# Two 32-expert layers of a transformer kernel: products in written order, weight slots by first release, 1664 expert slots instead of 1792

## The chip, the cores and the metric

One core of one Trainium2 chip runs the whole program in one launch. The metric is the device time of that launch in microseconds (us), as the median of several runs. The engines are PE (TensorE: products, with its weight loads as PEld), DVE (VectorE), ACT (ScalarE), POOL (GpSimd) and SP (SyncE, whose queue issues all weight transfers here). A megabyte (MB) is a million bytes.

## What is computed

The reference takes 512 tokens of width 1024 in float32. Block 1 ends in a layer of 16 experts. Block 2 has two depths, and each ends in a layer of 32 experts (4 groups of 8): a token's group is the largest group logit, its two experts are the two largest logits within it, and every expert applies `silu(x Wg) * (x Wu)` of width 512, then `Wd`. Cut to the part that the change touches:

```python
def _hier_moe(x, w_grp, b_grp, w_exp, b_exp, w_gate, w_up, w_down):
    ...
    g_idx = jnp.argmax(grp_logits, axis=-1)
    ...
    top_l, top_e = lax.top_k(in_grp, TOP_K_IN_GROUP)
    gate = p_grp[:, None] * jax.nn.softmax(top_l, axis=-1)
    eid = (g_idx[:, None] * EXPERTS_PER_GROUP + top_e).reshape(-1)
    ...
    def expert_block(args):
        idx, e = args
        xb = x_pad[idx]
        hdn = jax.nn.silu(xb @ w_gate[e]) * (xb @ w_up[e])
        return hdn @ w_down[e]
```

A layer so has 1024 pairs of token and expert, and the weights of its 32 experts are 32 x 3 x 512 x 1024 x 4 bytes, 201 MB.

## The kernel before, in words

`program()` runs block 1 (a mixer, a router, 16 experts), then twice a mixer, a router and a 32-expert layer. The two 32-expert layers share one function, `moe_sorted` (L491 to L626).

**Sorting and passes.** The number of pairs of an expert is known only on the chip. The router ranks the experts by it and writes the list `eids` (L1041): which expert stands at which place. The places are fixed ahead, by `_passes()` (L39 to L64). A place has one or two passes, and a pass is a number of rows (slots) that a product handles at once. Kind b, for the experts with the most pairs, has two passes of 64 and 32 rows; kind m has one of 64; kind s one of 32; kind f has one of 64 for an expert whose number is written in the program, so that its weights can be fetched before the list exists. Before there are `FIRST = 4` f, `BIG = 4` b, `MID = 12` m and 12 s: 36 passes, 1792 slots. Pairs that do not fit run in a loop behind the layer (`further`), whose count is read on the chip. Passes are collected into units of 128 slots (14 units), and units into groups of at most two units (7 groups).

**The weights.** All weights go through a ring of 12 slots of 1.049 MB each (`ring`, `slot()` L183, `load_w` L207). An expert needs six: gate 2, up 2, down 2, so the ring holds two experts. `fetch(x)` places expert x in slots 6x to 6x + 5, modulo 12, gate first; the fetch of expert x + 2 is written behind the last step of expert x. SP issues the transfers in this order, and its queue waits at each for the products that read the slot's old contents (L218 is the issue).

**A step.** For each pass (`step`): `pass_gates` (L652) sums the gate values of the unit's slots; `gate_up_64` (L664) or `gate_up_32` (L674) makes 64 products of 256 columns into a PSUM tile `pgu`; `hidden` applies silu and the gate; a share of `gather` (L274) collects the token columns of the next group into `xT`, 8 products for each of 8 blocks of 128; `hidden_T` (L344, L689) turns the hidden rows through the bank `ph`; the first pass of a unit then scatters the unit before (`scatter`, 8 tiles of two products at L392 into `psc`, each added to X by DVE at L395) and turns its one-hots into `ST`; `down` (L358) or `down_32` (L699) writes `py`, from where ACT and DVE copy it into a high part `Yh` (L372) and a low part `Yl` (L373).

**What sets the order.** The text order decides for SP, and within what the tile framework may move for the rest: PE's order in this function is chosen by a scheduler, which may let one step's products pass another's. `in_order()` is a context in which PE keeps the order written. The router's end, `router2`, writes `eids`, brings positions and gates into the order of passes (`by_pass`, L1062 and L1066) and works out the loop's count, all ahead of the first expert. `residual2` (L957, L958) scales X and adds a row, two DVE instructions for each of 4 token tiles; it is called from steps 0 and 1 and must precede the first scatter. `tokens2` gathers the first group's tokens ahead of the layer (L889 products, 256 columns each for four f experts; L282 and L284 modulate them into `xT`).

```python
        for x, mine in enumerate(EXPERTS):
            W = Ws[x % depth]
            ...
            for q in mine:
                step(q, W)
            fetch(x + depth)
```

Of the kernel before, what the change touches and what calls it, by code (L numbers as in the profile page):

```python
# [28 lines left out]
FIRST = 4  # L29
BIG, MID = 4, 12  # L30
# [8 lines left out]
def _passes():  # L39
# [5 lines left out]
    for g, units in enumerate((("ff", "ff"), ("bs", "mss"), ("mm", "mm"), ("bs", "mss"), ("bs", "mss"), ("mm", "mm"), ("bs", "mss"))):  # L45
        col = 0
        for u in units:
            for k in u:
                rank, low = next(kinds[k][0]), 0
                mine = []  # L50
                for size in kinds[k][1]:
                    mine.append(Pass(rank, size, low, g, unit, col))
                    col += size
                    low += size
                experts.append(mine)
                out += mine
            unit += 1
# [72 lines left out]
class Kernel:  # L130
# [57 lines left out]
    def new_ring(self):  # L188

        while self.rings:  # L190
            self.rings.pop().__exit__(None, None, None)
        for s in range(NSLOT):
            self.rings.append(self.tc.tile_pool(name=f"ring{s}", bufs=1))
            self.ring[s] = self.rings[s].__enter__()
# [12 lines left out]
    def load_w(self, src, n, inner=False):  # L207


        kt = src.shape[0] // 128  # L210
        per = SLOT // n
        out = []
        for k0 in range(0, kt, per):
            m = min(per, kt - k0)
# [46 lines left out]
    def onehot(self, g, tiles=range(NT)):  # L261

        V = self.nc.vector
        for k in tiles:
            V.tensor_tensor(self.S[g % 2][:, k].rearrange("p (e s) -> p e s", e=GRP), bc(self.c("slots"), GRP, 1),
                            bc(self.pos[:, k, g * GRP:(g + 1) * GRP], 64), OP.is_equal)
# [224 lines left out]
    def moe_sorted(self, weights, stats, finish, rows=()):  # L491
# [6 lines left out]
        depth = NSLOT // SLOTS  # L498
        last = PASSES[-1].group
        Ws = [None] * depth  # L500

        def load(e):
            W = []
            for m, w in enumerate(weights):
                w = w[e] if isinstance(e, int) else w[bass.ds(e, 1)].rearrange("o k n -> (o k) n")
                W.append(self.load_w(w, w.shape[1], m < 2))
            return W

        def fetch(x):

            if x < len(EXPERTS):
                self.wslot = SLOTS * x
# [5 lines left out]
                Ws[x % depth] = load(e)  # L518

        for x in range(depth):  # L520
            fetch(x)
        blocks = list(range(KD))

        def ahead(g, n):

            if g < last:
                for i in range(n):
                    self.gather(self.xT[(g + 1) % 2], S[(g + 1) % 2], blocks.pop(0))

        def step(q, W):  # L530
            g, i = q.group, q.i
            xq = xT[g % 2][:, :, q.col:q.col + q.size]
            if q.starts:
                blocks[:] = range(KD)
                if g < last:
                    self.onehots(g + 1)
            if q.opens and i:
                self.pass_gates(q)
            pg = self.gate_up_64(xq, W) if q.size == 64 else self.gate_up_32(xq, W)
            if i == 0:  # L540
                self.pass_gates(q)
            col = 4 * (q.unit % 2) + q.mates.index(q)
            hs = self.hidden(pg, col) if q.size == 64 else self.hidden_32(pg, col)
            n = q.size // 32 if g else (0, 2, 3, 3)[i]
            ahead(g, n // 2)
            hT = self.hidden_T(hs) if q.size == 64 else self.hidden_T_32(hs)
            if q.opens:
                if i:
                    for tt, n2 in tiles:
                        self.scatter(tt, n2, parts)  # L550
                p = self.slots_to_tokens(S[g % 2], q.col)
                nc.scalar.activation(self.ST, p, AF.Copy)
            ahead(g, n - n // 2)
            if i < 2:
                for t in (2 * i, 2 * i + 1):
                    self.residual2(t)
            r = slice(q.at, q.at + q.size)
            if q.size == 64:
                self.row = q.at // 64
                self.down(hT, W, self.Yh[r], self.Yl[r])  # L560
            else:
                self.down_32(hT, W, self.Yh[r], self.Yl[r])
# [43 lines left out]
        for x, mine in enumerate(EXPERTS):  # L606
            W = Ws[x % depth]
            if mine[0].starts and mine[0].group == last:
                self.rows = self.work[(last + 1) % 2]
                for t, r in zip(self.rows, rows):  # L610
                    self.bcast_into(t, r)
            for q in mine:
                step(q, W)
            fetch(x + depth)
        for tt, n in tiles:
            self.scatter(tt, n, parts)
# [11 lines left out]
    def onehots(self, g):  # L628

        V = self.nc.vector  # L630
        mine = [q for q in PASSES if q.group == g]
        i, n = mine[0].i, len(mine)
        for k in range(NT):
            pos = self.posp[:, k, i:i + n]
            out = self.S[g % 2][:, k]
            if n == 4:
                V.tensor_tensor(out.rearrange("p (e s) -> p e s", e=4), bc(self.c("slots"), 4, 1), bc(pos, 64), OP.is_equal)
            else:
                pos, out = pos.rearrange("p (u e) -> p u e", u=2), out.rearrange("p (u s) -> p u s", u=2)
# [2014 lines left out]
```

## Time and profile before

| | |
|---|---|
| runs | 2726.48, 2727.9, 2731.2 us; median 2727.9 |
| profiled execution | 2736.2 us; span in the trace 2734.4 us; mean granted PE clock 0.949 |
| busy PE | 2432.4 us (89%), 15602 products |
| busy PEld | 1510.4 us (55%) |
| busy DVE | 1203.9 us (44%) |
| busy ACT | 724.9 us (27%) |
| busy POOL | 284.7 us (10%) |
| transfers | 716.37 MB, mean 262 GB/s |

All positions are us from the start of the span of the one profiled execution. In the page's slices the span is cut into 40 equal parts. In a row of the trace, "64x512" is partitions x elements of the output, "x16" the number of instructions that the row collects, and what stands in brackets behind `<-` is the idle time of the engine and what ended it. "SPq" is SP's queue of transfers. A busy share is an average over stages with different limits, so a stage is read in its own window.

### The profile page before, as it was taken

To read this page: it belongs to the slowest core of one execution; us is meant where nothing else is said; L and a number is where in the kernel's file an instruction comes from. 1 tells how busy PE (TensorE), PEld (TensorE's weight loads), DVE (VectorE), ACT (ScalarE), POOL (GpSimd) and SP (SyncE) were. 2 spreads that over 40 slices of the span, in tenths; PEclk is the share of its full clock that TensorE was granted. 3 is DMA by queue.
4 is the path that set the end of the run, shared out by engine and by line. 5 is a ranking of instruction groups with operands and counts; after the bars stand their busy time and mean duration, and the time that the engine had idled before them with its cause. 6 is when DMAs were issued, how large, how long until landed. Compare 5 with 4: busy or idle time off the path is not lost. (4 is left out here: it accounts for less than half of the span.)

```text
span 2734.4 us, 39473 instructions
## 1 busy us (share of the span) xinstructions
PE 2432.4 (89%) x15602; PEld 1510.4 (55%) x15602; DVE 1203.9 (44%) x2706; ACT 724.9 (27%) x1512; POOL 284.7 (10%) x297
## 2 busy tenths in 40 slices
PE   7998996999998889998899988887978999998985
PEld 4876673443332367767666544545766755545542
DVE  4397566132221254576534333235464544333334
ACT  4452322110100043354212121114554212111111
POOL 1333231000000032110000000001440000000000
PEclk9999998999999999998899999998988999999997
DMA  7234736899999932012579999994101587989995
GB/s 264 76 112 141 252 108 239 339 409 409 409 409 409 403 120 69 24 34 95 216 310 415 397 369 392 417 366 154 46 24 35 200 332 318 417 346 407 416 367 213
DMA packets 202735, 716.37 MB, mean 262 GB/s; under 512 B 36553, under 2 KB 41577, under 8 KB 169770
## 3 DMA queue, kind: packets, MB, share of 16 engines
q1 hardware_dynamic: 202250, 713.62, 67.3%
q8 instruction: 129, 2.11, 0.3%
q14 instruction: 68, 0.56, 0.1%
q10 hardware_dynamic: 288, 0.08, 0.0%
HBM read 704.79 MB, written 8.86 MB: 261 GB/s over the span
## 5 line engine op out<-in xcount | busy, mean ns | idle before, releaser
L664 PE MATMUL pgu<-r,xT 128*64 128x256 f32 x2560 | 310.6, 390 | 0.0
L358 PE MATMUL py<-r,hT 128*64 128x512 f32 x1120 | 276.0, 619 | 15.2 <-ACT hT L346 15.1
L395 DVE TENSOR_TENSOR X<-X,psc 128x512 f32<-128x512 f32 x280 | 183.9, 685 | 204.0 <-PE psc L392 201.6
L664 PEld LDWEIGHTS pgu<-r,xT 128*64 128x64 f32 x2560 | 179.7, 139 | 107.9 <-issue 28.1
L324 PE MATMUL pgu<-r,xT 128*64 128x512 f32 x1024 | 235.2, 598 | 3.5 <-DMA r<-w_up_in 3.1
L373 DVE TENSOR_TENSOR Yl<-py,Yh 32x256 fp32r<-32x256 f32 (+1 forms) x208 | 109.1, 525 | 269.8 <-ACT Yh L372 268.6
L372 ACT ACTIVATE Yh<-py 32x256 fp32r<-32x256 f32 (+1 forms) x208 | 95.3, 458 | 306.6 <-PE py L358 151.2
L392 PE MATMUL psc<-Yh,ST 128*128 128x512 f32 x280 | 131.2, 471 | 36.6 <-ACT Yh L372 20.2
L358 PEld LDWEIGHTS py<-r,hT 128*64 128x64 f32 x1120 | 77.0, 140 | 152.0 <-issue 123.1
L1128 DVE TENSOR_TENSOR wl<-r,wh 128x512 fp32r<-128x512 f32 (+2 forms) x154 | 119.5, 790 | 91.5 <-ACT wh L1124 85.2
L1159 PE MATMUL pj<-wl,ah 128*128 128x512 f32 (+1 forms) x384 | 155.3, 405 | 2.4 <-DVE wl L1128 2.4
L1159 PE MATMUL pj<-wh,ah 128*128 128x512 f32 (+1 forms) x384 | 151.9, 415 | 5.0 <-DVE cv L1320 2.6
L1159 PE MATMUL pj<-wh,al 128*128 128x512 f32 (+1 forms) x384 | 151.0, 399 | 0.0
L324 PEld LDWEIGHTS pgu<-r,xT 128*64 128x64 f32 x1024 | 68.8, 137 | 136.8 <-issue 121.5
L1124 ACT ACTIVATE wh<-r 128x512 fp32r<-128x512 f32 (+2 forms) x168 | 97.7, 596 | 169.8 <-PE pj L1159 116.9
L274 PE MATMUL pg<-S,xh 128*128 128x256 f32 x512 | 135.6, 295 | 4.0 <-DVE xT L284 3.1
L223 POOL TENSOR_TENSOR lnmv<-lnmv,mhalf 128x1 f32<-128x1 f32 x16 | 10.4, 652 | 1235.0 <-DVE lnmv L722 1224.5
L335 ACT ACTIVATE hs<-pgu 128x256 f32<-128x256 f32 (+1 forms) x56 | 25.0, 446 | 411.4 <-PE pgu L664 274.5
L274 PE MATMUL pg<-S,xl 128*128 128x256 f32 x512 | 133.9, 292 | 0.0
L336 DVE SCALAR_TENSOR_TENSOR hs<-hs,gs,pgu 128x256 f32<-128x256 f32 (+1 forms) x56 | 31.1, 555 | 231.1 <-ACT hs L335 231.0
L674 PE MATMUL pgu<-r,xT 128*32 128x256 f32 x2048 | 126.8, 381 | 2.3 <-SPq L619 1.7
L392 PE MATMUL psc<-Yl,ST 128*128 128x512 f32 x280 | 121.6, 437 | 1.7 <-DVE Yl L373 1.3
(733 smaller groups left out, 4099.0 us busy)
## 6 DMA issues: line engine op xcount, KB each, us to landing
r<-moe_w_gate_in SPq DMA_DIRECT2D x128, 1024.0 KB
r<-moe_w_up_in SPq DMA_DIRECT2D x128, 1024.0 KB
r<-moe_w_down_in SPq DMA_DIRECT2D x128, 1024.0 KB
r<-w_down_in SPq DMA_DIRECT2D x64, 1024.0 KB
r<-w_up_in SPq DMA_DIRECT2D x64, 1024.0 KB
r<-w_gate_in SPq DMA_DIRECT2D x64, 1024.0 KB
r<-w_mod_in SPq DMA_DIRECT2D x24, 1024.0 KB
r<-ev_w_in_in SPq DMA_DIRECT2D x14, 1024.0 KB
```

Of the source, the lines that this page charges most:

```text
L274: nc.tensor.matmul(p, part[:, k, d * 128:(d + 1) * 128], S[:, k], start=(k == 0 and part is self.xh), stop=(k == NT - 1 and part is self.xl))
L324: nc.tensor.matmul(pg[64 * h:64 * h + 64, which, :], xT[:, k, j, :], w[:, h * H:(h + 1) * H], start=(k == 0 and (F == 1024 or which == 0)) ...
L358: nc.tensor.matmul(py[64 * n:64 * n + 64], hT[:, b, hf, :], w[:, n * 512:(n + 1) * 512], start=(hf == 0 and b == 0), stop=(hf == 1 and b = ...
L372: nc.scalar.activation(hi, p, AF.Copy)
L373: nc.vector.tensor_tensor(lo, p, hi.bitcast(F32), OP.subtract)
L392: nc.tensor.matmul(p, ST[:, tt * 128:(tt + 1) * 128], Y[:, n * 512:(n + 1) * 512], start=(i == 0), stop=(i == len(parts) - 1))
L395: nc.vector.tensor_tensor(a, a, p, OP.add)
L664: nc.tensor.matmul(pg[64 * h:64 * h + 64, which, :], xq[:, k], W[which][k][:, h * H:(h + 1) * H], start=(k == 0 and which == 0), stop=(k = ...
L674: nc.tensor.matmul(pg[32 * c:32 * c + 32], xq[:, k], W[1 - c // 2][k][:, c % 2 * H:(c % 2 + 1) * H], start=(k == 0), stop=(k == KD - 1), s ...
L1124: self.nc.scalar.activation(wh, w, AF.Copy)
L1128: eng.tensor_tensor(wl, w, wh.bitcast(F32), OP.subtract)
L1159: nc.tensor.matmul(banks[m], a, b, start=(k == 0 and j == 0), stop=(k == KD - 1 and j == 2))
```

## The change

The slots of a layer go from 1792 to 1664: `FIRST` 4 to 2, `BIG` 4 to 3, so there are 2 f, 3 b, 12 m and 15 s, 35 passes in 13 units. The experts from place 2 on come from the list; before, from place 4 on.

The step of a pass is split by expert into `front(x)` and `back(x)`. `front` makes gate and up of all the expert's passes side by side: the first half of the k blocks for both passes, then the second half, and it applies silu and gate. `back` turns the hidden rows, scatters the unit before with the gather blocks between its tiles (one after every two), and makes the down products. The order is front(x), back(x - 1), the fetch of down(x + 1), the fetch of gate and up of x + 2. The whole runs under `in_order()`. The gates of a unit are made behind the back that precedes it. In an expert with two passes `down_32` uses the bank `ph` in place of `py`.

The weights of gate and up are loaded as gate half 0, up half 0, gate half 1, up half 1. The slot of each load comes from a list worked out ahead (`free`): slots in the order in which the program gives them back, the four of a front behind that front, the two of a down behind its back. `new_ring(place)` lets the next mixer find its slots under this order.

In `router2` and behind it: the list is written in `numbers()`, called between the two halves of front(0); positions and gates come into pass order in `permute()`, behind front(0). The eight `residual2` instructions are called behind experts 1 and 2. The first group is gathered 128 columns wide instead of 256. The next group's one-hots are made for all four token tiles in one instruction per part.

```diff
-FIRST = 4
-BIG, MID = 4, 12
+FIRST = 2
+BIG, MID = 3, 12
...
-    for g, units in enumerate((("ff", "ff"), ("bs", "mss"), ("mm", "mm"), ("bs", "mss"), ("bs", "mss"), ("mm", "mm"), ("bs", "mss"))):
+    for g, units in enumerate((("ff",), ("mss", "mss"), ("bs", "mss"), ("mm", "mm"), ("bs", "mss"), ("mm", "mss"), ("bs", "mss"))):
...
+        def gate_up_weights(ws):
+
+            W = [[], []]
+            for k in range(0, KD, 4):
+                for m in range(2):
+                    W[m] += self.load_w(ws[m], ws[m].shape[1], True, range(k, k + 4))
+            return W
...
+        n, G = len(EXPERTS), SLOTS - SLOTS // 3
+        order = list(self.order)
+        free = list(order)
+        for x in range(n + 1):
+            free += order[SLOTS * x:SLOTS * x + G] + (order[SLOTS * x - SLOTS // 3:SLOTS * x] if x else [])
+            order += free[len(order):SLOTS * min(n, x + 3)]
+        self.freed = free[-NSLOT:]
+        self.set_order(order)
...
+        def front(x):
+
+            mine, W = EXPERTS[x], Ws[x]
+            q = mine[0]
+            if q.starts and x and q.group < last:
+                self.onehots(q.group + 1)
+            make = {64: self.gate_up_64, 32: self.gate_up_32}
+            pg = [self.mps.tile([128, 2, self.F // 2], F32, name="pgu", bufs=2) for m in mine]
+            for k in range(0, KD, 4):
+                for m, p in zip(mine, pg):
+                    make[m.size](p, xT[q.group % 2][:, :, m.col:m.col + m.size], W, range(k, k + 4))
+                if x == k == 0:
+                    self.numbers()
+            if x == 0:
+                self.permute()
+                self.onehots(1)
                 self.pass_gates(q)
...
+        def back(x, hs, blocks, g):
...
+            chores = [lambda t=t: self.scatter(*t, parts) for t in tiles] if q.opens and x else []
+            for i, d in enumerate(blocks):
+                chores.insert(3 * i + 2 if len(chores) > i else i, lambda d=d: gather(g, d))
...
+                    self.down(h, W, self.Yh[r], self.Yl[r])
+                else:
+                    self.down_32(h, W, self.Yh[r], self.Yl[r], "ph" if two else "py")
...
+        with self.in_order():
+            hs = None
+            for x, mine in enumerate(EXPERTS):
...
+                new = front(x)
+                if x:
+                    back(x - 1, hs, share.get(q.i, []), q.group + 1)
+                    fetch_down(x + 1)
+                fetch_gate_up(x + 2)
+                hs = new
+                if x in (1, 2):
+                    for t in (2 * x - 2, 2 * x - 1):
+                        self.residual2(t)
+                if x + 1 < n and EXPERTS[x + 1][0].opens:
+                    self.pass_gates(EXPERTS[x + 1][0])
+            back(n - 1, hs, [], None)
```

The order of instructions shows three places. The first is PE at the start of the first 32-expert layer. Names: `place` is the permutation, `own` belongs to the loop's count, `pos` and `gate` are the positions and gates brought into pass order, `r_` are weight slots. Before:

```order
L1040 MATMUL py<-place,C 1x36
L1062 MATMUL pg<-C,pos 32x128 x4
L1066 MATMUL pg<-place,xT_8615 128x36 x4
L1053 MATMUL py<-own,C 128x32
L1062 MATMUL pg<-C,gate 32x128 x4
L1066 MATMUL pg<-place,xT_8615 128x36 x4
L2629 UNCONDITIONAL_BRANCH
L664 MATMUL pgu<-r_8998,xT_8614 64x256 x8
L664 MATMUL pgu<-r_8999,xT_8614 64x256 x8
```

And of the change, from the last pair of the first half of expert 0 on:

```order
L722 MATMUL pgu<-r_8996,xT_8613 64x256 x2
L722 MATMUL pgu<-r_8997,xT_8613 64x256 x2
L1103 MATMUL py<-place,C 1x35
L722 MATMUL pgu<-r_8998,xT_8613 64x256 x2
L722 MATMUL pgu<-r_8999,xT_8613 64x256 x2
...
L1127 MATMUL pg<-C,pos 32x128 x4
L1131 MATMUL pg<-place,xT_8614 128x35 x4
L1127 MATMUL pg<-C,gate 32x128 x4
L1131 MATMUL pg<-place,xT_8614 128x35 x4
L1117 MATMUL py<-own,C 128x32
L711 MATMUL ph<-gate_9127,S_8615 128x4 x4
L722 MATMUL pgu<-r_9001,xT_8613 64x256 x2
```

The list's product now stands behind half of expert 0's gate and up, and the permutation behind all of it.

The second is DVE at the same place, in the change. Before, the cast into `eids` (L1041) is followed by the branch, and the residual comes within the layer:

```order
L1098 TENSOR_SCALAR own<-C,sortc 32x32
L2695 UNCONDITIONAL_BRANCH
L1043 SCALAR_TENSOR_TENSOR X<-X,resg 128x1024
L1044 SCALAR_TENSOR_TENSOR X<-resb,X 128x1024
...
L1071 MEMSET turnx 128x1
L1072 MEMSET turnx 128x1
L1104 CAST eids<-py 1x35
L1111 TENSOR_TENSOR posp<-pg,low 128x140
```

Four such pairs at L1043 and L1044 now stand ahead of the cast that SP reads its expert numbers from.

The third is PE behind an expert with 96 rows, in the change: the last scatter tile, the two downs, the turning of the one-hots (`identr`), the gates of the next unit, and the next front:

```order
L393 MATMUL psc<-Yh,ST 128x512
L393 MATMUL psc<-Yl,ST 128x512
L359 MATMUL py<-r_9001,hT 64x512 x4
L359 MATMUL py<-r_9002,hT 64x512 x4
L754 MATMUL ph<-r_9001,hT 32x256 x8
L754 MATMUL ph<-r_9002,hT 32x256 x8
L308 MATMUL psc<-identr,S_8615 128x128 x4
L711 MATMUL ph<-gate_9127,S_8615 128x6 x4
L722 MATMUL pgu<-r_8998,xT_8613 64x256 x2
```

The gates write `ph` right behind the down that wrote it, and every later product stands behind them; before, the scheduler had set 64-row gate-up products between such steps.

## Rows read from the trace of the kernel before

**Rows 1.** The page's slices of 68.4 us, the row of GB/s that the transfers moved.

```profile
GB/s 264 76 112 141 252 108 239 339 409 409 409 409 409 403 120 69 24 34 95 216 310 415 397 369 392 417 366 154 46 24 35 200 332 318 417 346 407 416 367 213
```

**Rows 2.** Windows: stretch, us, busy PE, PEld, DVE, ACT, POOL (count), PEclk, DMA, GB/s.

```profile
1349.00:1849.00 500.00, 456.50 (x3836) 259.54 (x3836) 176.71 (x396) 92.92 (x208) 0.00 (x0) 0.99 0.93 378
2194.00:2697.00 503.00, 459.48 (x3854) 260.71 (x3850) 176.49 (x397) 93.31 (x209) 0.00 (x0) 0.99 0.94 378
1440.00:1560.00 120.00, 114.88 (x892) 68.41 (x891) 43.45 (x105) 23.31 (x50) 0.00 (x0) 1.00 1.02 417
500.00:920.00 420.00, 390.71 (x1781) 149.87 (x1779) 98.25 (x174) 45.67 (x76) 0.00 (x0) 0.99 1.02 406
```

**Rows 3.** SP's longest sum of waits, 1300 to 1870 us: total us, times, longest.

```profile
SPq L218 <- PE pgu L674: 103.1, 24, 21.6
```

**Rows 4.** Timeline of SP's queue: start us, us, issues.

```profile
1347.16 2.41 SPq L218 DMA_DIRECT2D r<-moe_w_gate_in  x2
...
1407.21 2.10 SPq L218 DMA_DIRECT2D r<-moe_w_down_in  x2
1430.19 2.07 SPq L218 DMA_DIRECT2D r<-moe_w_gate_in  x2
```

**Rows 5.** Timeline of PE within the first layer: start us, us, line, operation.

```profile
1439.12 0.39 PE L274 MATMUL pg<-S,xh 128*128 128x256 f32 x1
...
1440.26 0.65 PE L664 MATMUL pgu<-r,xT 128*64 128x256 f32 x2
...
1444.08 6.69 PE L664 MATMUL pgu<-r,xT 128*64 128x256 f32 x58
...
1833.41 3.65 PE L358 MATMUL py<-r,hT 128*64 128x512 f32 x16 [0.53 <-ACT hT L346]
1836.99 3.66 PE L674 MATMUL pgu<-r,xT 128*32 128x256 f32 x64
1841.66 0.34 PE L689 MATMUL ph<-C,hs 64*128 64x64 f32 x2 [1.01 <-DVE hs L682]
1842.42 1.93 PE L699 MATMUL py<-r,hT 128*32 128x256 f32 x32 [0.43 <-ACT hT L691]
```

**Rows 6.** Timeline of PE, ACT and DVE at the start of the first layer.

```profile
1326.16 0.56 PE L889 MATMUL po<-S,xh 128*128 128x256 f32 x1
...
1331.08 0.52 PE L923 MATMUL lg<-M,onesr 128*128 128x32 f32 x4
...
1335.00 1.02 ACT L282 ACTIVATE xT<-S,pcol 128x256 f32<-128x256 f32 x2
1336.38 0.18 DVE L1041 CAST eids<-py 1x36 int32<-1x36 f32 x1 [0.37 <-PE py L1040]
1343.44 9.22 PE L664 MATMUL pgu<-r,xT 128*64 128x256 f32 x64
```

**Rows 7.** Groups by line: residual; copies of down. Busy us, mean ns, idle before.

```profile
L957 DVE SCALAR_TENSOR_TENSOR X<-X,resg 128x1024 f32<-128x1024 f32 x4 | 4.9, 1220 | 0.0
...
L373 DVE TENSOR_TENSOR Yl<-py,Yh 64x512 fp32r<-64x512 f32 x10 | 6.9, 688 | 16.1 <-ACT Yh L372 16.1
L372 ACT ACTIVATE Yh<-py 64x512 fp32r<-64x512 f32 x10 | 5.9, 592 | 19.2 <-PE py L358 15.4 <-DVE Yl L373 3.8
```

**Rows 8.** Timeline of DVE at the end of the two layers.

```profile
1864.36 1.35 DVE L395 TENSOR_TENSOR X<-X,psc 128x512 f32<-128x512 f32 x2 [0.16 <-PE psc L392]
...
2701.54 0.42 DVE L373 TENSOR_TENSOR Yl<-py,Yh 32x256 fp32r<-32x256 f32 x1 [0.44 <-ACT Yh L372]
```

**Rows 9.** Timeline of PE, the last products of the two layers.

```profile
1865.44 0.40 PE L392 MATMUL psc<-Yl,ST 128*128 128x512 f32 x1
...
2711.18 0.63 PE L392 MATMUL psc<-Yl,ST 128*128 128x512 f32 x1
```

**Rows 10.** Windows, columns as in Rows 2: the layer's start, and a stretch within it.

```profile
1320.00:1360.00 40.00, 33.01 (x188) 26.13 (x190) 25.30 (x94) 8.02 (x16) 0.00 (x0) 0.72 0.36 135
1740.00:1780.00 40.00, 34.26 (x210) 16.74 (x210) 10.45 (x25) 5.11 (x11) 0.00 (x0) 1.00 1.02 416
```

More of the change, by code (lines that the diff above doesn't have):

```diff
@@ L517, in fetch @@
                                        skip_runtime_bounds_check_because="the list holds the numbers of the experts, by their places")
[L518 to L537, printed above, removed]
-                self.pass_gates(q)
[L539 to L546, printed above, removed]
@@ new lines, in fetch_gate_up, with fetch_down, gather, shares @@
+                source[x] = matrices(e)
+                Ws[x] = gate_up_weights(source[x]) + [None]
+        def fetch_down(x):
+            if x < n:
+                w = source.pop(x)[2]
+                Ws[x][2] = self.load_w(w, w.shape[1])
+        for x in range(2):
+            fetch_gate_up(x)
+            fetch_down(x)
+        def gather(g, d):
+            self.gather(self.xT[g % 2], S[g % 2], d)
+        def shares(g):
+            mine = [e for e in EXPERTS if e[0].group == g]
+            if g == last:
+                return {}
+            if g == 0:
+                return {mine[1][0].i: list(range(KD))}
+            out, blocks = {e[0].i: 1 for e in mine}, list(range(KD))
+            for e in [e for e in mine if not e[0].opens] + mine:
+                if sum(out.values()) < KD:
+                    out[e[0].i] += 1
+            assert sum(out.values()) == KD
+            return {i: [blocks.pop(0) for d in range(c)] for i, c in out.items()}
@@ L547, in step @@
             if q.opens:
[L548 to L551, printed above, removed]
+                p = self.slots_to_tokens(S[q.group % 2], q.col)
                 nc.scalar.activation(self.ST, p, AF.Copy)
[L553 to L557, printed above, removed]
@@ L604, in further @@
                 self.scatter(tt, n, [(self.ST[:64], self.Yh[:64]), (self.ST[:64], self.Yl[:64])])
[L606 to L616, printed above, removed]
+        with self.in_order():
+            hs = None
+            for x, mine in enumerate(EXPERTS):
+                q = mine[0]
+                if q.starts:
+                    share = shares(q.group)
+                    if q.group == last:
+                        self.rows = self.work[(last + 1) % 2]
+                        for t, r in zip(self.rows, rows):
+                            self.bcast_into(t, r)
+                new = front(x)
[10 more added lines that the diff above has]
+            back(n - 1, hs, [], None)
+        for t in tiles:
+            self.scatter(*t, parts)
         v = nc.values_load(self.nover[0:1, 0:1], min_val=0, max_val=15,
@@ L856, in tokens2 @@
         pl = ps.tile([128, 512], F32, name="lg", bufs=1)
[L857 to L858 removed]
+        acc = [ps.tile([128, 512], F32, name="tr", bufs=2) for n in range(2)]
+        n0 = FIRST * 64
+        part0 = lambda d: acc[d // 4][:, d % 4 * n0:d % 4 * n0 + n0]
         E = 32
@@ L917, in tokens2 @@
                 (gather, 0), (gather, 1), (rank, 2), (logits, 3), (gather, 2))
-            acc.append(ps.tile([128, 512], F32, name="S0", bufs=2))
-            for t in range(3):
-                gather(t, (6, 7))
             for t in range(NT):
@@ L924, in tokens2 @@
             rank(3)
-            gather(3, range(KD))
+            gather(3)
             self.count = mp.tile([128, E], F32, name="count")
```

158 lines of the change are left out of this document (84 added, 74 removed).

## The prediction

> **What bounds the kernel now.** I read the page's slices first, to find the two 32-expert layers: the GB/s row climbs to 415, stays near 400 and falls to 46, and climbs a second time to 417, in slices 20 to 28 and 32 to 40 of 68 us each [rows 1]. But for the gather just ahead of them the rest of the program is written as before, so only these two stretches count. Then the table by stage. In the first layer 500 us, from 1349 to 1849 us, move 378 GB/s, that is 189 MB: the 180 loads of 1.049 MB (188.7 MB) that follow the 12 already in the ring. The second layer does the same in 503 us. But where the transfers run without a break, over 120 us of the first layer, they move 417 GB/s [rows 2]. At 417 the 180 loads take 452.6 us (2.51 us each, 15.1 an expert), so each layer has 47 to 50 us of holes in its transfers. PE is busy 456 of the 500 us [rows 2]: nearly as much of a bound. The two alternate: three experts of few rows load longer (45 us) than they compute, two of many rows compute longer than they load (30 us).
>
> Who makes the holes, SP's own waits say: around the first layer it stood 103 us for 32-row gate-up products alone to free a slot, 21.6 us once [rows 3]. The largest hole is seen in SP's order: a pair of down loads at 1407.2, the next pair only at 1430.2 [rows 4]. That is an expert with 96 rows: its two passes run one after the other, and the queue's next gate load needs a slot that the second pass still reads. So the holes are a matter of when slots are given back, not of the memory.
>
> **The change, part by part.**
>
> *PE's work.* From the rows: 64-row gate-up has 58 of its 64 instructions in 6.69 us, so some 7.3 for all; 32-row gate-up 3.6; 64-row down 3.6; 32-row down 1.9; a gather block 1.14 [rows 5]. One scatter tile is two products of 512 columns, 0.23 us each as in the 64-row down, 0.47; gates and transposes of a unit some 2, as an estimate from 0.34 for one of them. A unit of 128 slots is then 14.6 + 7.3 + 4 x 1.14 + 8 x 0.47 + 2 = 32 us of PE. Before there were 14 units a layer, now 13 (1664 slots): 420 us instead of 452. Taken alone this buys nothing where weights are awaited; it moves PE clearly below the 453 us of loads.
>
> *The start of a layer.* Now the sorted list (eids) is written at 1336.4, PE works on the permutation until 1343.4 and only then starts the first gate-up, 9.2 us at a slow clock; the first load goes out at 1347.2 [rows 4, 6] and lands from 1349 on. The last modulate ends at 1336.0, on 256 columns. Ahead of it 24 gather products of 256 columns hold PE from 1326.2 to the count at 1331.1 [rows 6]; now they are 16 of 128, by width a third, 1.6 us instead of 4.9, and the last gather and the modulates are half as wide. The mask that the count needs takes part of this back, so I take 3 us: gate-up starts near 1333 and gives a slot back near 1338. But experts 2 and 3 now need the list too, and DVE has the eight residual instructions ahead of the cast: 8 x 1.22 = 9.8 us from about 1333.8 [rows 7], so the list is there at 1343.6 and SP issues near 1345. Most of the earlier start is given back: the transfers restart 2 us sooner than now, at 1347 and, in the second layer, counted from its present start of 2194, at 2192. Bounds: 8 us sooner still (no residual ahead of the cast), 5 later.
>
> *Slots by first release, gate and up by halves, down behind the next front.* A gate-up slot is now free after half a front, and the next load in line takes whichever slot is free first. By hand over the first experts: loads of expert 2 run 1347 to 1357 in expert 0's slots, its down and half of expert 3 to 1367 in expert 1's; the other half waits for expert 0's down, which stands behind front 1 and all 64 gather products, near 1371 (PE: 1333 + 9.2 + 7 of permutation + 7.3 + 9.1 + 3.6 + some 2 of waits). A hole of 4 us. Later an expert of 96 rows gives half its slots back 5.5 us after it starts, with six slots loaded or loading beside it (15 us), so the 21 us hole goes. The two "mm" units need 34 us of PE for 30 of loads and may leave another 4. I take 8 us of holes per layer, with 0 and 25 as ends.
>
> *What written order adds.* PE can no longer fill a wait with another product. The scatter is paced by DVE (a pair in 1.35 us after a hand-over of 0.16, so 0.75 a tile) against 0.47 of PE [rows 8]; two gather blocks stand between to cover some: of the 2.3 us a unit 1 is left, 13 a layer. After a 96-row expert the gate products of the next unit wait for the bank that down wrote: four parts follow each other at 0.86 us [rows 8] behind two of 0.59 + 0.69 us [rows 7], 6 us less the 2.4 that PE still has to do: 4 us, three times a layer. Transposes behind their hidden rows cost 1.0 us of PE idle where nothing is between [rows 5]; now a whole front is. With 10 us for the rest PE needs 420 + 35 = 455 us from 1333, to 1788, and would be idle some 35 us for weights. ACT and DVE work is below half the time [rows 2]. The 28 more SP instructions lie in SP's waits.
>
> *The end.* The last load is a down, then one 32-row down and eight scatter tiles, as now: 1849 to 1865.8 and 2697 to 2711.8 [rows 9]; kept at 17 and 15.
>
> **Sum.** First layer: 1347 + 452.6 + 8 + 17 = 1824.6 instead of 1865.8: -41. Second: 2192 + 452.6 + 8 + 15 = 2667.6 instead of 2711.8: -44. The profiled execution, 2736.2, becomes 2651; it lies 8.3 over the median of 2727.9, so the forecast is **2643 us**. About 0.2% (5 us) is what measuring this kernel can tell from no change.
>
> **Rivals.**
> 1. *PE's waits become the bound.* If the covers fail, a unit adds 2.3 us of scatter and 3.6 of transposes (two or three of 1.0 + 0.43), with the gates 88 us a layer: 420 + 88 = 508 from 1333, end at 1841, -25 a layer: 2678. For it: written order has nothing to put in a wait. Against: a front stands between. Chance 0.20.
> 2. *No holes at all*, and the cast slips ahead: restart 1339, end 1809, -57 a layer: 2614. Chance 0.07.
> 3. *The memory does not hold 417.* If a closed hole only lowers the rate to today's mean of 378, the 500 us stay: 2728, no change. Against it, besides the 417, the 16-expert layer: 406 over 420 us [rows 2]. The Trainium skill, DMA: Bandwidth & Descriptors, section Specifications, gives about 358 GB/s as one core's limit from HBM; by it 189 MB would take 527 us and no order of slots could help. By that rule today's 500 us could not be; the trace disagrees. Chance 0.03.
> 4. *Slower: the clock.* PE now waits for weights at the head of its order, and a granted clock that falls in these waits makes PE the bound. With PE's 420 us at full clock and 35 of waits from 1333, the layer ends behind today's 1866 once its mean clock is under 0.84; at 0.80 it ends at 1893, +27 a layer: 2782. The trace: 0.72 at the layer's start, with 33 of 40 us busy and little dense work; but 1.00 with 34.3 of 40 busy [rows 10], and PE would be busy about 0.88. The Trainium skill, TensorE: Matmul & The Clock Gate, Part 1, says the slow level is the default and activity releases it, which speaks against any change that makes PE wait; the first of these rows agrees with it, the second does not bear it out. Chance 0.04.
> 5. *A further pass runs.* The sorted experts from the 16th on hold 32 rows instead of 64; counting the reference's routing on these inputs, the 16th largest count is 24 in the first layer and 32, just full, in the second. One more pair there and one pass of the loop behind the layer runs: six loads with nothing beside them (15 us) and 25 of PE. 2643 + 40 = 2683. Chance 0.04.
>
> **Numbers.** The forecast's case has 0.62. Rivals 1, 2 and 5 are faster too: 0.62 + 0.20 + 0.07 + 0.04 = 0.93; the same 0.03; slower 0.04. The range reaches from nearly no holes (2614) to holes of 25 us a layer (2643 + 34 = 2677), rival 1 and a restart at its later end: 2616 to 2688.
>
> **What would show it.** Right: 417 GB/s with holes of under 10 us from the restart to the last load, near 1347 and 2151 (the second layer starts 41 us earlier); last products near 1824 and 2627; PE waits on weights at the fronts. Wrong: the transfers idle over 25 us in a layer (rival 1), granted clock under 0.9 (rival 4), work in the loop behind the layer (rival 5), or a restart before 1342.

## The result and the profile after

The changed kernel takes 2662.7 us (median of 4 runs, 2660.3 to 2665.6) beside 2729.6 for the kernel before (4 runs, 2726.5 to 2732.6): a ratio of 0.9756, 95% interval 0.9739 to 0.9772, so 67 us faster. Forecast were 2643, within 2616 to 2688. The profiled execution took 2661.8 us, 74.4 less than the one before (2736.2). It is 1 us under its median; the one before was 8.3 over the median of the three runs then on record (2727.9) and is 6.6 over that of four (2729.6).

From the page: the span, the busy time of each engine, and the row that answers to [rows 1].

```profile
span 2659.6 us, 39104 instructions
PE 2355.1 (89%) x15454; PEld 1491.1 (56%) x15454; DVE 1178.2 (44%) x2618; ACT 718.5 (27%) x1510; POOL 284.2 (11%) x297
GB/s 265 83 104 131 266 131 244 275 409 409 409 409 409 409 230 80 48 35 33 206 278 417 416 417 401 417 416 201 64 24 36 206 224 416 416 417 405 417 416 185
```

The valleys within the two layers are gone: 417, 416, 417, 401, 417, 416 stands where 415, 397, 369, 392, 417, 366 stood. The table by stretch, columns as in [rows 2]: the two stretches of transfers, and what follows the last load of each layer.

```profile
1346.00:1808.00 462.00, 416.79 (x3697) 248.56 (x3700) 161.40 (x360) 88.89 (x203) 0.00 (x0) 0.95 1.00 408
2152.00:2616.00 464.00, 415.59 (x3716) 247.89 (x3720) 161.94 (x361) 89.06 (x204) 0.00 (x0) 0.96 1.00 408
1808.00:1831.00 23.00, 14.89 (x112) 7.24 (x100) 9.23 (x17) 3.92 (x11) 0.00 (x0) 0.78 0.05 20
2616.00:2638.00 22.00, 13.69 (x104) 6.58 (x96) 9.26 (x17) 3.92 (x11) 0.00 (x0) 0.77 0.08 30
```

The same 180 loads now take 462 and 464 us instead of 500 and 503. What got longer is the end: from the last load to the last product it is 22 and 21 us instead of 17 and 15.

SP's sums of waits over the first layer (total us, times, longest), to set beside [rows 3]:

```profile
SPq L219 <- PE pgu L722: 72.6, 26, 10.1
SPq L219 <- PE py L359: 68.8, 26, 9.2
...
SPq L219 <- PE pgu L730: 33.8, 17, 5.9
SPq L534 <- DVE eids L1104: 33.1, 1, 33.1
```

The waits for 32-row gate-up products sum to 33.8 us where they were 103, and the longest is 5.9 us where it was 21.6. The longest for 64-row products is 10.1. PE's groups by line, 1346 to 1835 us, with the idle time ahead of each and what ended it:

```profile
L722 PE MATMUL pgu<-r,xT 128*64 128x256 f32 x1024 | 132.5, 419 | 15.2 <-DMA r<-moe_w_up_in 9.8 <-DMA r<-moe_w_gate_in 5.2
L730 PE MATMUL pgu<-r,xT 128*32 128x256 f32 x1152 | 70.3, 392 | 12.3 <-DMA r<-moe_w_up_in 12.3
...
L393 PE MATMUL psc<-Yh,ST 128*128 128x512 f32 x104 | 47.9, 462 | 7.9 <-DVE X L396 4.8 <-ACT Yh L373 3.0
...
L711 PE MATMUL ph<-gate,S 128*128 128x6 f32 (+1 forms) x52 | 8.9, 276 | 11.3 <-DVE Yl L374 10.8 <-DVE gate L1115 0.5
```

PE now waits for weights, 27.5 us in the fronts of the first layer. The waits that written order adds are there too, and small: 7.9 at the scatter (3.0 of them, for copies of ACT, stand behind the last load), 10.8 at the gates.

### The profile page after: what moved, and what is told of

The parts are those of the page before. It is cut to its first block, busy times and chain, and to the rows that moved or that the text cites. A ratio compares the mean times of both kernels' runs of the same rounds, so it can differ in the third digit from the quotient of the medians.

```text
span 2659.6 us, 39104 instructions
## 1 busy us (share of the span) xinstructions
PE 2355.1 (89%) x15454; PEld 1491.1 (56%) x15454; DVE 1178.2 (44%) x2618; ACT 718.5 (27%) x1510; POOL 284.2 (11%) x297
## 5 line engine op out<-in xcount | busy, mean ns | idle before, releaser
L722 PE MATMUL pgu<-r,xT 128*64 128x256 f32 x2176 | 282.8, 420 | 35.1 <-DMA r<-moe_w_up_in 22.1
L359 PE MATMUL py<-r,hT 128*64 128x512 f32 x1024 | 238.8, 609 | 8.9 <-ACT hT L347 8.9
L722 PEld LDWEIGHTS pgu<-r,xT 128*64 128x64 f32 x2176 | 166.4, 152 | 138.9 <-issue 33.2
L396 DVE TENSOR_TENSOR X<-X,psc 128x512 f32<-128x512 f32 x264 | 170.8, 683 | 70.7 <-PE psc L393 70.2
L374 DVE TENSOR_TENSOR Yl<-py,Yh 32x256 fp32r<-32x256 f32 (+1 forms) x188 | 97.4, 518 | 226.3 <-ACT Yh L373 225.2
L373 ACT ACTIVATE Yh<-py 32x256 fp32r<-32x256 f32 (+1 forms) x188 | 85.0, 452 | 324.4 <-PE py L359 202.5
L730 PE MATMUL pgu<-r,xT 128*32 128x256 f32 x2304 | 139.7, 390 | 26.3 <-DMA r<-moe_w_up_in 25.0
L359 PEld LDWEIGHTS py<-r,hT 128*64 128x64 f32 x1024 | 69.9, 139 | 141.2 <-issue 124.0
L325 PEld LDWEIGHTS pgu<-r,xT 128*64 128x64 f32 x1024 | 68.7, 136 | 136.6 <-issue 122.5
L393 PE MATMUL psc<-Yh,ST 128*128 128x512 f32 x264 | 120.7, 459 | 20.5 <-DVE X L396 14.4
L336 ACT ACTIVATE hs<-pgu 128x256 f32<-128x256 f32 (+1 forms) x50 | 22.6, 452 | 416.8 <-PE pgu L722 279.7
L730 PEld LDWEIGHTS pgu<-r,xT 128*32 128x32 f32 x2304 | 71.6, 112 | 88.2 <-DMA r<-moe_w_up_in 32.1
```

The source lines that it names most:

```text
L325: nc.tensor.matmul(pg[64 * h:64 * h + 64, which, :], xT[:, k, j, :], w[:, h * H:(h + 1) * H], start=(k == 0 and (F == 1024 or which == 0)) ...
L359: nc.tensor.matmul(py[64 * n:64 * n + 64], hT[:, b, hf, :], w[:, n * 512:(n + 1) * 512], start=(hf == 0 and b == 0), stop=(hf == 1 and b = ...
L373: nc.scalar.activation(hi, p, AF.Copy)
L374: nc.vector.tensor_tensor(lo, p, hi.bitcast(F32), OP.subtract)
L393: nc.tensor.matmul(p, ST[:, tt * 128:(tt + 1) * 128], Y[:, n * 512:(n + 1) * 512], start=(i == 0), stop=(i == len(parts) - 1))
L396: nc.vector.tensor_tensor(a, a, p, OP.add)
```

## The experiments

Theory 1 was the prediction's: transfers set a layer's length, and the holes between them closed because slots come back in time. Theory 2: PE sets it, and the 128 slots fewer are the gain. Differences below are between medians, against 2662.7. Each run also has its ratio to the kernel before on its own chip, with a 95% interval; where this overlaps the changed kernel's (0.9739 to 0.9772), a difference is not shown.

**e1: slots in fixed order.**

```diff
-        self.freed = free[-NSLOT:]
-        self.set_order(order)
+        base = list(self.order)
+        self.freed = base[:G] + base[SLOTS:SLOTS + G] + base[G:SLOTS] + base[SLOTS + G:]
+        self.set_order(base)
```

> The changed kernel with one part undone: the slots go round in fixed order (an expert in the same six as two experts before), where the changed kernel takes the slot that is free first. Theory 1 (the transfers set a layer's length, and first release closes their holes): each pair of down loads now waits until the back two experts earlier is done, so holes return in part, 10 to 30 us a layer, and the run takes 20 to 60 us more than the changed kernel's 2662.7, 2683 to 2723. Theory 2 (PE sets the length, and the time came from the 128 slots fewer): within 5 us of 2662.7.

Measured: 2715.6 us, ratio to before 0.9938 (0.9922 to 0.9955): 53 us slower than the changed kernel. SP's waits in the first layer:

```profile
SPq L219 <- PE py L359: 173.8, 26, 22.5
SPq L219 <- PE py L755: 115.9, 26, 13.0
```

Now it is the downs for which SP waits: those of 64 rows (L359) 173.8 us in all and 22.5 once, where it was 68.8 and 9.2. Theory 1 holds, theory 2 falls. Of the 67 us, 14 are left.

**e2: 1792 slots in the new order.**

```diff
-BIG, MID = 3, 12
+BIG, MID = 3, 16
...
-(("ff",), ("mss", "mss"), ("bs", "mss"), ("mm", "mm"), ("bs", "mss"), ("mm", "mss"), ("bs", "mss"))
+(("ff",), ("mm", "mss"), ("bs", "mm"), ("mm", "mm"), ("bs", "mss"), ("mm", "mm"), ("bs", "mss"), ("mss",))
```

> The changed kernel with 1792 slots again: 16 places of 64 rows and 11 of 32 in place of 12 and 15, 14 units instead of 13, one more last group; everything else as in the changed kernel. It adds some 32 us of PE work to each layer and no load. Theory 1: PE waited 27 us on loads in the first layer's fronts, so most of the added work goes into these waits: 10 to 35 us more than 2662.7 over both layers, 2673 to 2698. Theory 2: all of it shows, 64 us or more, 2727 and up.

Measured: 2681.2 us, 0.9828 (0.9808 to 0.9849): 18.5 us slower. PE's waits for weights over 1350 to 1819 us show where half of the added PE work, an estimated 32 us a layer, went:

```profile
PE pgu L730 <- DMA r<-moe_w_up_in: 7.7, 3, 4.2
PE pgu L722 <- DMA r<-moe_w_up_in: 4.0, 3, 1.8
```

They fall from 27.5 to 12 us. So, next to the rest of the change, the 128 slots are worth about 9 us a layer, not 32 and not nothing; where the other 7 or 8 went was not traced.

**e3: less PE work.** The low part of the gathers is left out in these two layers.

```diff
-            self.gather(self.xT[g % 2], S[g % 2], d)
+            p = self.mps.tile([128, 512], F32, name="pg", bufs=2)[:, :256].rearrange("p (e s) -> p e s", e=GRP)
+            for k in range(NT):
+                nc.tensor.matmul(p, self.xh[:, k, d * 128:(d + 1) * 128], S[g % 2][:, k], start=(k == 0), stop=(k == NT - 1))
+            self.modulate(d, self.xT[g % 2][:, d], p, d % 2)
```

> The changed kernel without the low part of the gathers inside the two 32-expert layers (192 products of 256 columns a layer left out, so gathered tokens lose their low bits): some 23 us less PE work a layer at the dense rate, no load changed. Theory 1: the loads still take 452.6 us, only PE's lag at the end shrinks: 0 to 12 us less than 2662.7 in all. Theory 2: 40 us or more less, 2620 or below.

Measured: 2661.9 us, 0.9748 (0.9732 to 0.9765): no difference is shown, and PE waits longer for weights instead, 36.2 us:

```profile
L725 PE MATMUL pgu<-r,xT 128*64 128x256 f32 x1024 | 133.9, 422 | 20.3 <-DMA r<-moe_w_up_in 13.0 <-DMA r<-moe_w_gate_in 7.3
L733 PE MATMUL pgu<-r,xT 128*32 128x256 f32 x1152 | 72.6, 401 | 15.9 <-DMA r<-moe_w_up_in 14.6 <-SPq L683 1.2
```

In the profiled executions the two layers are some 5 and 3 us shorter, from the first issue behind the list to the last product, and the mixer between them some 5 us longer. So of an estimated 23 us of PE work a layer at most 3 to 5 show: the changed layer is bound by its transfers.

**e4: the passes in turn.**

```diff
-            for k in range(0, KD, 4):
-                for m, p in zip(mine, pg):
+            for m, p in zip(mine, pg):
+                for k in range(0, KD, 4):
...
```

> The changed kernel with the two passes of a 96-row expert one after the other (all of gate and up of the first pass, then of the second) instead of side by side. Its slots come back 5.5 us later at three places a layer. Theory 1, if the six other slots do not cover it: 3 to 6 us of holes at each place, 10 to 30 us more than 2662.7. If they cover it (15 us of loads are under way): within 5 us. Theory 2: within 5 us, since PE's work is the same.

Measured: 2659.3 us, 0.9737 (0.9721 to 0.9753). Its interval overlaps with the changed kernel's (0.9739 to 0.9772): side by side buys nothing that can be measured here. SP's waits for 32-row gate-up products do grow, from 33.8 to 43.7 us and the longest from 5.9 to 9.4, but the transfers still move 408 GB/s over 462 us: the other slots under way cover them.

**e5: order left to the scheduler**, all else as changed.

```diff
-        with self.in_order():
+        if True:
             hs = None
```

> The changed kernel without the pinned order of PE: front, back, slots and table as they are, but the scheduler may let products pass each other. Theory 1 (transfers bound, PE has slack): the order matters only where it delays the release of a slot; -5 to +25 us against 2662.7. Theory 2' (pinned order is itself worth much, because the scheduler's order interleaves products so that slots are read longer): 2690 or more. If pinned order costs PE waits that matter: 2655 or less.

Measured: 2747.1 us, 1.0049 (1.0032 to 1.0066): 84 us slower than the changed kernel and slower than the kernel before. I had put at most 25 on this at theory 1. The timeline of PE, where SP issues nothing between 1456 and 1475:

```profile
1462.83 0.65 PE L722 MATMUL pgu<-r,xT 128*64 128x256 f32 x4
...
1464.54 1.20 PE L393 MATMUL psc<-Yh,ST 128*128 128x512 f32 x2 [1.06 <-ACT Yh L373]
...
1468.10 4.86 PE L722 MATMUL pgu<-r,xT 128*64 128x256 f32 x28
1472.89 1.93 PE L730 MATMUL pgu<-r,xT 128*32 128x256 f32 x32
```

And SP's queue, then its two largest sums of waits, 1318 to 1830 us:

```profile
1456.44 0.33 SPq L219 DMA_DIRECT2D r<-moe_w_up_in  x1
1474.89 0.96 SPq L219 DMA_DIRECT2D r<-moe_w_down_in  x2
```

```profile
SPq L219 <- PE pgu L722: 167.4, 25, 13.5
SPq L219 <- PE pgu L730: 116.6, 23, 17.9
```

The scheduler starts a front with 4 of its 32 products in a gap of the scatter, goes back to the scatter, which waits for ACT and DVE, and makes the other 28 some 5 us later. The 32-row products of the same front follow at 1472.9, and SP's longest wait, 17.9 us, ends with them. The slots that the front reads stay taken as long. In all, SP waits 284 us for gate-up products in place of 106: filling PE's gaps costs SP its slots. How much of the 84 us is due to fronts torn like this one was not measured.

**e6: no lookahead.** The expert's back directly behind its front, with e1's slots.

```diff
-                new = front(x)
-                if x:
-                    back(x - 1, hs, share.get(q.i, []), q.group + 1)
-                    fetch_down(x + 1)
+                back(x, front(x), share.get(q.i, []), q.group + 1)
                 fetch_gate_up(x + 2)
...
+                fetch_down(x + 2)
...
-            back(n - 1, hs, [], None)
```

> The changed kernel with back(x) right behind front(x), in place of back(x - 1): down of an expert directly behind its own gate and up, pinned order, residual one expert earlier. Release order is then the order of loading, so the slots go round in the fixed order, which is here the order of first release. Theory 1: PE waits at each expert for silu, gate and turning (1.0 + 0.43 us and more, some 60 to 80 us a layer over 35 passes), of which 27 us are free: 20 to 80 us more than 2662.7, PE being the bound again. Rival (the wait is covered by the scatter and gathers that stand between): within 10 us.

Measured: 2670.8 us, 0.9775 (0.9760 to 0.9790): 8 us slower by the medians, at the rival's end of what was expected; by the ratios it is 5, and the intervals overlap. With back behind front the fixed order is already the order of release, and the transfers hold 404 GB/s (the first layer, 1352 to 1817):

```profile
1352.00:1817.00 465.00, 407.97 (x3718) 241.10 (x3718) 164.24 (x363) 90.80 (x208) 0.00 (x0) 0.98 0.99 404
```

So the list of first release is needed because the down was moved behind the next front; the two come as a pair, and the pair is worth 5 to 8 us if anything.

**e7: the list ahead of the residual**, and **e8: also the first down ahead of the gathers.** e7 holds each residual behind the last DVE instruction written before it:

```diff
+        traced = self.nc.cur_bb.bb.instructions
+        m, before = len(traced), [i for i in traced if i.engine == mybir.EngineType.DVE][-1]
         self.nc.vector.scalar_tensor_tensor(x, x, ALPHA, g, op0=OP.mult, op1=OP.mult)
+        self.behind([i for i in traced[m:] if i.engine == mybir.EngineType.DVE][0], before)
```

> The changed kernel with the eight residual instructions of DVE held behind the work of the first experts, so that they no longer stand ahead of the cast into the list. The list is there 3.5 us sooner (1339.6 instead of 1343.2) and the transfers restart as much sooner, at about 1342. If the restart sets the layer: 7 us less in all, 2656. If the next slots decide: the hole at 1367 to 1371, which ends when the down of expert 0 behind 64 gather products gives its slots back, grows by the same 3.5 us, and the run stays within 3 us of 2662.7. I hold the second for likelier.

e8 adds:

```diff
+            late = []
+            if x == 0:
+                chores, late = [], chores
             for i, f in enumerate(chores):
...
                 nc.scalar.activation(self.ST, p, AF.Copy)
+            for f in late:
+                f()
```

> e7 and the down of expert 0 ahead of the 64 gather products of its back instead of behind them, so that its two slots come back some 9 us sooner and the hole at 1367 closes. If restart and this hole set the layer: 3.5 + 3.5 us a layer, 14 us less, 2649. If PE's place at the end of the layer decides (it was behind the loads there): 0 to 6 us less.

Measured: 2662.6 us, 0.9745 (0.9732 to 0.9758), and 2663.9 us, 0.9751 (0.9738 to 0.9764): no difference from the changed kernel for either. SP's waits in e7's first layer:

```profile
SPq L219 <- PE py L359: 79.5, 26, 11.9
...
SPq L534 <- DVE eids L1107: 29.4, 1, 29.4
```

The wait for the list is 3.7 us shorter, and the wait for downs 10.7 longer. In e8 the wait moves on to the gate-up products:

```profile
SPq L219 <- PE pgu L727: 85.6, 27, 11.5
```

At a layer's start the ring is full and PE gives the slots back, so an earlier first load only brings the next wait forward.

**e9: the kernel before, with pinned order.**

```diff
+        with self.in_order():
             for x, mine in enumerate(EXPERTS):
...
                 for q in mine:
                     step(q, W)
                 fetch(x + depth)
```

(The lines of the loop only move in by a level.)

> The kernel before with one edit: the loop over the experts runs in the order written (its steps, table, slots and loads are as they were). Theory A, formed on e5 and e6 (pinned order is what closes the holes: each expert's slots are given back when its own step ends, and the scheduler no longer stretches the reads of one expert over the next): e6's 2670.8 plus e2's 18.5 for the 128 slots, 2685 to 2705. Theory B (the prediction's: the holes come from the fixed slots and the passes in turn, and pinned order only adds PE waits): 2728 to 2760.

Measured: 2714.1 us, 0.9935 (0.9918 to 0.9952): 16.5 us faster than before. Neither theory's numbers hold it. Pinned order alone helps the old kernel, where the prediction knew it as a cost; but the hole behind the 96-row expert stays, as SP's queue shows (before: 1407.21 and 1430.19 in [rows 4]):

```profile
1409.57 2.10 SPq L218 DMA_DIRECT2D r<-moe_w_down_in  x2
1433.24 2.07 SPq L218 DMA_DIRECT2D r<-moe_w_gate_in  x2
```

In e6, whose slots go round in fixed order too, that hole is gone. SP's waits for 32-row gate-up products in the first layer, e9 and then e6:

```profile
SPq L218 <- PE pgu L675: 90.4, 22, 21.0
```

```profile
SPq L219 <- PE pgu L727: 21.3, 17, 5.1
```

So pinned order alone does not close this hole, and the list of first release is not needed for it. e6 differs from e9 in the loads by halves with the passes side by side, in the 128 slots and in the order of steps; these were not undone one by one.

**e10: fixed slots and the scheduler's order**, the edits of e1 and e5 together.

> e5 (order of PE left to the scheduler) with the slots in fixed order as in e1. If e5 was slow because the list of first release was worked out for the written order and did not fit the order in which the scheduler gave slots back: clearly under e5's 2747, 2700 to 2730. If the scheduler's order is slow by itself: 2740 or more.

Measured: 2774.2 us, 1.0152 (1.0126 to 1.0177). The scheduler's order is slow by itself; the list was no hindrance to it but a help of 27 us. In a table (us):

| | slots by first release | fixed slots |
|---|---|---|
| written order | 2662.7 | 2715.6 |
| scheduler's order | 2747.1 | 2774.2 |

**e11: the last down in another bank**, and **e12: also the back of expert 30 ahead of the front of expert 31.**

```diff
-                    self.down_32(h, W, self.Yh[r], self.Yl[r], "ph" if two else "py")
+                    self.down_32(h, W, self.Yh[r], self.Yl[r], "ph" if two or x == n - 1 else "py")
```

> The changed kernel with the down of the last expert in the bank ph instead of py, so that it no longer waits 3.3 us for the copies of the down before it. That stands on the chain behind the last load in both layers: 2.5 to 3.3 us a layer, 2656 to 2658. If the copies by ACT and DVE decide there: within 2 us of 2662.7.

```diff
+                if x == n - 1:
+                    back(x - 1, hs, [], None)
                 new = front(x)
-                if x:
+                if 0 < x < n - 1:
```

> e11 and the back of expert 30 ahead of the front of expert 31, so that the last load is not followed by two downs. After the last load there are then a front of 32 rows, turning, one down and the scatter. The tail falls from 22 us to 17 or 18 a layer: 2653 to 2656. If only the scatter and the copies decide: as e11.

Measured: e11 2658.2 us (2657.0 to 2660.8 in 5 runs), 0.9735 (0.9721 to 0.975); e12 2665.2 us (2658.9 to 2672.8), 0.9762 (0.9741 to 0.9783). e11's median is 4.5 us lower, as expected, though the two intervals overlap, so the gain is not shown by the times alone; it has the lowest median, level with e4. e12 missed. PE at the end of the first layer, first the changed kernel, then e11, then e12:

```profile
1805.68 3.66 PE L730 MATMUL pgu<-r,xT 128*32 128x256 f32 x64
...
1810.15 1.93 PE L754 MATMUL py<-r,hT 128*32 128x256 f32 x32 [0.54 <-ACT hT L746]
...
1815.61 3.44 PE L754 MATMUL py<-r,hT 128*32 128x256 f32 x32 [3.27 <-DVE Yl L374]
...
1829.77 0.40 PE L393 MATMUL psc<-Yl,ST 128*128 128x512 f32 x1
```

```profile
1814.39 1.93 PE L754 MATMUL ph<-r,hT 128*32 128x256 f32 x32 [0.53 <-ACT hT L746]
...
1827.42 0.39 PE L393 MATMUL psc<-Yl,ST 128*128 128x512 f32 x1
```

```profile
1809.66 3.21 PE L756 MATMUL py<-r,hT 128*32 128x256 f32 x32 [2.00 <-ACT hT L748]
1812.58 4.16 PE L732 MATMUL pgu<-r,xT 128*32 128x256 f32 x64
1817.74 0.33 PE L746 MATMUL ph<-C,hs 64*128 64x64 f32 x2 [1.00 <-DVE hs L739]
```

In e11 the wait of 3.27 us is gone, and its down takes 1.93 us instead of 3.44. In e12 PE waits 2.00 us for a copy of ACT, the down behind it takes 3.21 us instead of 1.93, the front 4.16 instead of 3.66, and the last turning has nothing in front of it: what the shorter chain gives, the waits take back. From the first issue behind the list to the last product the layer takes 486 us, 482 (e11) and 486 (e12).

## Why the prediction was right, and which terms were off

The measured 2662.7 us lie within the range, 20 us over the forecast, and the transfers set the layer's length as forecast. Several terms were off, though, and the start came out right by luck.

- **The bound.** That transfers would set the layer, at 417 GB/s but for 8 us of holes, is what the trace and e3 show: restart at 1346 (predicted 1347), last load at 1808 (predicted 1347 + 452.6 + 8 = 1808). In the second layer 2152 (predicted 2151) and 2616 (predicted 2612). Rivals 1 to 5 did not come: the mean clock is 0.95 and 0.96 over the transfers, and there is no work in the loop behind the layer. Of rival 3: 408 GB/s held over 462 us. The Trainium skill, DMA: Bandwidth & Descriptors, section Specifications, gives about 358 GB/s as one core's limit from HBM; these 462 us do not bear it out as a limit for this run.
- **The start: right in position by luck.** The list came at 1343.4 (predicted 1343.6), because of the residual instructions ahead of it, and the transfers restarted near 1346. But the stretch ahead began 3.5 us earlier in this execution. The first gather product stands at 1311.5, before at 1315.0; in the traces of e1 to e8 and e10 to e12, with the same program up to there, it stands anywhere from 1312.6 to 1322.4. Counted from this product, SP's first issue behind the list comes after 32.6 us where it was 32.2, and in the second layer after 32.2 where it was 30.4. So the 2 us sooner did not come: in its own stage the start was 2.5 and 3.8 us later than reckoned. The gather term was mis-sized. The 16 products ahead of the count were put at 1.6 us; they issue 0.21 us apart, 3.5 in all. The last 16 behind the count also take 3.5, where 16 of 256 columns took 2.0 at the full clock (both below). So PE starts 22.6 us after the first gather product, at 1334.1; the last modulate had ended 21.0 us after it, and 3 less was reckoned. e7 and e8 show that the time of the list decided nothing. The first gather product before and after, then PE, the last residual and the list after:

```profile
1315.01 0.37 PE L889 MATMUL po<-S,xh 128*128 128x256 f32 x1
```

```profile
1311.49 0.31 PE L945 MATMUL tr<-S,xh 128*128 128x128 f32 x1
...
1334.12 5.29 PE L722 MATMUL pgu<-r,xT 128*64 128x256 f32 x32 [1.72 <-ACT xT L283]
...
1342.01 1.22 DVE L1044 SCALAR_TENSOR_TENSOR X<-resb,X 128x1024 f32<-128x1024 f32 x1
...
1343.17 0.18 DVE L1104 CAST eids<-py 1x35 int32<-1x35 f32 x1
```

- **The end: the term that failed.** "The last load is a down, then one 32-row down and eight scatter tiles, as now", kept at 17 and 15, took no account of its own change. With down behind the next front, PE is still in the last front (1805.7 to 1809.3) when the last load lands, just behind 1808; two downs follow, and the second waits 3.27 us for the bank of the first. Last products end at 1830.2 and 2636.9 instead of 1824.6 and 2627. In the second layer the end is 6 us longer than reckoned, the transfers 3.4, and the restart is 1 late: 10 of the 10.8 us by which the profiled execution (2661.8) missed its forecast (2651). The 5.6 us of the first layer do not come back in the second's restart: from the last product to the restart the mixer between takes 322 us where it took 328, and only 2 of that were reckoned. What was gained lies ahead of the second layer's first gather product, 287.6 us behind the last product where it was 295.8; its cause was not examined, so that the second restart fits is luck as well.
- **The median.** The 8.3 us between the profiled execution before and its median were taken off the forecast as well. The profiled execution after has no such distance, so the forecast in medians lost another 7 to 9 us: 2643 against 2662.7.
- **Written order.** Its costs were sized well or too high: 10.8 us at the gates (predicted 4 us three times), 7.9 at the scatter (13), 27.5 us of waits for weights (35). But the prediction knew it only as a cost. e5 and e10 show that without it the new program is slower than the old one; what it gives, an early end of each front's reads, had no term.
- **Slots by first release, and side by side.** The hole of 21 us is gone. The reason given, slots that come back in time, holds: with fixed slots and the down behind the next front 53 us come back (e1). But the list is needed only in this order of steps, since e6 closes the hole without it. The two passes side by side have no share that can be measured next to the list (e4).
- **The 128 slots.** "Taken alone this buys nothing where weights are awaited": e2 measures 9 us a layer. PE's slack is not everywhere: in e2's first layer SP waits 107.1 us for 64-row downs and 95.6 for 64-row gate-up, in place of 68.8 and 72.6. Which units make PE late there was not traced.

What stays open: e9 and e6 lie 43 us apart; 18.5 of that are the slots by e2's price, and the rest (loads by halves, passes side by side with fixed slots, gathers between the scatter tiles, the start of the layer, place of the gates) was not taken apart. So that transfers bound the layer and that the holes closed is shown; which part of the change closed the largest is not.

## What to carry to other kernels

Where a ring of buffers feeds an engine, ask of every reordering when each buffer's last reader ends: a scheduler that fills the engine's gaps with a few products of the next step holds that step's buffers, and the transfers pay for it. Price the parts of a change as pairs: slots by first release cost at most some 8 us to do without while the down follows its own front (e6), and 53 us once it doesn't (e1). When work is moved behind the next stage, work out the end of the layer again, since what was hidden under loads has nothing above it there.

## What was not expected of the hardware

Half the columns made these gather products no shorter at the low clock. Ahead of the first layer the granted clock is 0.50 both where the kernel before makes 256 columns (1326 to 1330 us) and where the changed one makes 128 (1328.7 to 1332.2). They follow each other 0.21 us apart in both, first before, then after:

```profile
1327.16 0.41 PE L889 MATMUL tr<-S,xh 128*128 128x256 f32 x1
1327.37 0.41 PE L889 MATMUL tr<-S,xl 128*128 128x256 f32 x1
```

```profile
1329.00 0.41 PE L945 MATMUL tr<-S,xl 128*128 128x128 f32 x1
1329.21 0.41 PE L945 MATMUL tr<-S,xh 128*128 128x128 f32 x1
```

At the full clock, 1.00, there is hardly more in it: 0.12 us apart with 256 columns, 0.11 with 128:

```profile
1333.13 0.28 PE L889 MATMUL po<-S,xh 128*128 128x256 f32 x1
1333.25 0.28 PE L889 MATMUL po<-S,xl 128*128 128x256 f32 x1
```

```profile
1311.75 0.27 PE L945 MATMUL tr<-S,xh 128*128 128x128 f32 x1
1311.86 0.27 PE L945 MATMUL tr<-S,xl 128*128 128x128 f32 x1
```

Each product has a load of 128 x 128 weights of its own, and its record did not shrink with the columns: 0.33 us at the low clock and 0.19 at the full one, in both kernels. That the load sets the pace is argued from these rows and was not tried by itself. Only the lower count, 16 instead of 24, made the part ahead of the count shorter (3.5 us instead of 4.9). The part behind it became longer, 3.5 us instead of 2.0, since it now ran at 0.50 where it had run at 1.00.

The granted clock is a little lower over the transfers, 0.95 and 0.96 where the kernel before had 0.99 [rows 2]. That this comes from PE's waits for weights is argued, not shown. PE had time to spare there (e3), so it cost little. Behind the last load it is 0.78 (0.70 before), and there it shows on the chain: a down takes 3.44 us right behind a wait of 3.27 (the changed kernel) and 3.21 behind one of 2.00 (e12), in place of 1.93.
